# Block 2's first weight chunk split earlier, two modulation units moved ahead, low-part terms last in a three-term product

## The chip, the cores and the metric

The kernel runs on one core of a Trainium2 chip. The metric is the device time of one execution in microseconds (us). The engines are named as in the profile: PE is the matrix engine (PEld its weight loads), DVE the vector engine, ACT the scalar engine, POOL the general-purpose engine, SP the queue that issues nearly all loads.

## The reference, cut to what matters

Two blocks run one after the other on 256 tokens of width 1024 in float32. The first block ends in a mixture of 32 experts, two per token. The second block has two layers; each starts with a normalisation that is scaled and shifted by a modulation vector, and a product with `w_in`.

```python
for e in range(N_EXPERTS):                                   # end of block 1
    he = jax.nn.silu(h @ w_gate[e]) * (h @ w_up[e])
    y = y + comb[:, e:e + 1] * (he @ w_down[e])
x = rms_norm(x + y, final_norm_g)
...
c_act = jax.nn.silu(c)
for l in range(DEPTH_2):                                     # block 2, two layers
    mod = c_act @ w_ada[l] + b_ada[l]
    shift, scale, gate = jnp.split(mod, 3, axis=-1)
    h = rms_norm_2(x, norm_g[l]) * (1.0 + scale[:, None, :]) + shift[:, None, :]
    u = h @ w_in[l]
    rg_x, rg_z, ml_x, ml_o, ml_z = jnp.split(u, split_pts, axis=-1)
    ...
    x = x + gate[:, None, :] * (y @ w_out[l])
```

## The kernel before, in words

**Products in three terms.** Activations and weights are split into a high part (rounded to the fast float32 format) and a low part (the rest). A product is the sum high times high, high times low and low times high, so that each tile costs three matmuls (`mm3`, lines 265 to 272). A weight chunk of 1 MB (`col_chunk`, 1024 rows by 256 columns) is split by `split_cols` in two units of 128x1024: ACT copies the high part (`wh`, line 282) and DVE subtracts it (`wl`, line 283). Three buffers each hold `wh` and `wl`. The last chunk of a stage, which is needed right after it, is split into two buffers of the weight pool instead; such tiles are called `wo`.

**Weight buffers.** The pool `wp` has 8 buffers of 1 MB and serves nearly all loads; the pool `we` has 5 more and lives only as long as the experts. Expert weights come in 96 chunks of 1 MB, six for a pair of experts: four of gate and up weights (`g`), two of down weights (`d`). They are dealt over 17 buffers in turn: 5 of `we`, 8 of `wp`, 4 others. The last six chunks (two of pair 15's gate and up chunks, the two down chunks of pair 14 and the two of pair 15) lie in `wp`. Their loads are kept in program order on SP.

**The expert stage.** There are 16 pairs. For each, PE multiplies the gathered tokens with gate and up weights (line 1165), ACT and DVE form the hidden values (lines 1169 and 1170), PE turns them (line 1114) and multiplies them with the down weights (line 1122), ACT and DVE split the result (lines 1124 and 1125), and PE scatters it back to tokens (`back`, line 1135), where DVE adds it to `x1` (line 1137).

**From experts to block 2.** After the pairs, `head_load(0)` loads block 2's first weight chunk into `wp` and splits it into two `wo` buffers (4 splits: two on ACT, two on DVE). The last `back` adds to `x1`; `head_scale` takes for each half of the tokens (i = 0, 1) two sums of squares on ACT (line 365) and two weighted sums on DVE (line 330), and the scale follows on DVE and POOL (lines 331 to 333 and 373). Sixteen matmuls without use for the result (`warm(16)`, line 355) stand behind the last `back` on PE, then one modulation unit. Then `Head(0)` scales `x1` to `xn` (lines 1228 and 1230), PE turns it (line 1236), and `evac` applies the modulation and splits the result in `hh` and `hl` (lines 1250 to 1261). Then `tm_product` computes the first product of block 2 for i = 0 and 1 (`gz0`, line 1291).

**Modulation units.** `ada_unit` computes 512 of the 3072 columns of `mod` of one layer: two 1 MB loads, 8 matmuls of 32 output rows each, which the trace records as 16 (line 401), and a copy on ACT (line 403). `ada_fold` adds four partial rows with 4 small matmuls, recorded as 8 (line 421), and writes shift and scale for the head with one or two small DVE operations (lines 423 and 425). Units 0 to 3 of a layer are folded and must be ready before that layer's head, units 4 and 5 feed the gate. Layer 1's unit 0 runs in the gap between experts and block 2, its units 1, 2 and 3 in layer 0's last stage (`out_proj`), one `unit()` call after each chunk.

**Products with tokens as the stationary side.** `tm_product(i, f)` serves `gz0` and seven more 256-column chunks in each layer (`gz` and `og`, line 1451). A chunk is used twice, for i = 0 and i = 1, each 24 matmuls over k = 0 to 7; k = 0 to 3 read the chunk's first unit, k = 4 to 7 its second.

**Order.** A planner simulates the program, takes for each engine the earliest ready instruction in program order, and so fixes the order in each engine's queue; `issue_after(x)` ties instructions behind x on their engine. On the chip each engine then takes its queue in that order.

Of the kernel before, what the change touches and what calls it, by code (L numbers as in the profile page):

```python
# [9 lines left out]
F32 = mybir.dt.float32  # L10
# [6 lines left out]
P = 128  # L17
T = 256
D = 1024
KT = 8  # L20
# [158 lines left out]
def model(ctx, tc, A, out, dbg=None):  # L179
# [10 lines left out]
    def nm(s):  # L190
        uid[0] += 1
        return f"{s}_{uid[0]}"

    def psum(tag="mm", bufs=4):
        return pp.tile([P, 512], F32, tag=tag, name=nm(tag), bufs=bufs)
# [56 lines left out]
            TE.matmul(o, lhsT=onesr, rhs=dg[:, 0:n].rearrange("p v t -> p (v t)"), start=j == 0, stop=j == 1)  # L252


    def wload(src, n, rows=P):

        t = wp.tile([P, 2048], F32, tag="w", name=nm("w"))
        shp = list(src.shape)
        v = t[:rows, :n]
        if len(shp) == 3:  # L260
            v = v.rearrange("p (a b) -> p a b", a=shp[1])
        SY.dma_start(out=v, in_=src)
        return t
# [123 lines left out]
    cact = cp.tile([P, KT], F32, name="cact")  # L387
    mods = [cp.tile([P, 16], F32, name=f"mods{l}") for l in range(2)]

    def ada_load(l, c):  # L390
        return [wload(A["w_ada_2"][l][hf * 512:(hf + 1) * 512, c * 512:(c + 1) * 512].rearrange("(k p) c -> p k c", p=P), 2048) for hf in range(2)]

    def ada_unit(pool, l, c, ws=None, a=None):


        if a is None:
            a = pool.tile([P, 512], F32, tag="ada", name=nm("ada"), bufs=2)
        acc = psum()
        for hf, w in enumerate(ws or ada_load(l, c)):
            for k in range(4):  # L400
                r = TE.matmul(acc[32 * k:32 * k + 32, :], lhsT=cact[:, hf * 4 + k:hf * 4 + k + 1].to_broadcast([P, 32]), rhs=w[:, k * 512:(k + 1) * 512],  # L401
                              start=hf == 0, stop=hf == 1)
        S.activation(out=a, in_=acc, func=AF.Copy)
        if ws is None:
            ada_fold()
        if c < 4:
            folds.append((l, c, a))
        else:
            gates.append(a)
        return r  # L410

    folds, gates = [], []

    def ada_fold():

        if not folds:
            return
        l, c, a = folds.pop()
        pt = psum_t()
        for j in range(4):  # L420
            TE.matmul(pt[:, j:j + 1], lhsT=a[:, j * P:(j + 1) * P], rhs=cc("r32"), start=True, stop=True)
        m = mods[l][:, 4 * c:4 * c + 4]
        V.tensor_tensor(out=m, in0=pt[:, 0:4], in1=vc(f"bad{l}", 4 * c, 4), op=OP.add)
        if c in (2, 3):
            V.scalar_tensor_tensor(out=m, in0=m, scalar=1.0, in1=vc(f"ng{l}", 4 * (c - 2), 4), op0=OP.add, op1=OP.mult)
# [60 lines left out]
    def eloads(n):  # L486
        while nslot[0] < min(n, len(chunks)):
            eload()
# [477 lines left out]
    with moe, tc.tile_pool(name="mo", bufs=1, reuse_waits="tile") as bp:  # L966
# [173 lines left out]
            return r  # L1140

        for pair in range(NP):
            eloads(6 * pair + 23)
            ws = loaded["g", pair]
            xg = xgs[pair]

            slot = cc("slot")[:, pair:pair + 1]
            oa = bp.tile([P, T], F32, tag="oa", name=nm("oa"))
            ohs = bp.tile([P, T], F32R, tag="ohs", name=nm("ohs"), bufs=3)
            wsl = bp.tile([P, 2], F32, tag="wsl", name=nm("wsl"), bufs=2)  # L1150
            for j in range(2):
                V.scalar_tensor_tensor(out=oa, in0=bc[:, j, :], scalar=slot, in1=bc[:, 2 + j, :], op0=OP.is_equal, op1=OP.mult, accum_out=wsl[:, j:j + 1])
            V.tensor_tensor(out=wsl[:, 0:1], in0=wsl[:, 0:1], in1=wsl[:, 1:2], op=OP.add)
            V.tensor_scalar(out=oa, in0=bc[:, 0, :], scalar1=slot, scalar2=None, op0=OP.is_equal)
            V.scalar_tensor_tensor(out=ohs, in0=bc[:, 1, :], scalar=slot, in1=oa, op0=OP.is_equal, op1=OP.add)

            gu = psum_a()
            for k in range(KT):
                for q in range(2):
                    o = q * CAP  # L1160
                    if pair:
                        w = ws[2 * (k // 4) + q][:].rearrange("p (g k c) -> p g k c", g=2, k=4)[:, :, k % 4, :]
                    else:
                        w = ws[k // 2][:].rearrange("p (q g k c) -> p q g k c", q=2, g=2, k=2)[:, q, :, k % 2, :]
                    r = TE.matmul(gu[64 * q:64 * q + 64, :], lhsT=xg[:, k, o:o + CAP], rhs=w, start=k == 0, stop=k == KT - 1)  # L1165
                    if pair < 2 and k + q:
                        tc.keep_in_program_order(r)
            sil = bp.tile([P, T], F32, tag="sil", name=nm("sil"), bufs=2)
            S.activation(out=sil, in_=gu[:, 0:256], func=AF.Silu)  # L1169
            V.scalar_tensor_tensor(out=sil, in0=gu[:, 256:512], scalar=wsl[:, 0:1], in1=sil, op0=OP.mult, op1=OP.mult)  # L1170
            hidden[pair] = sil, ohs
            if pair > 1:
                with tc.issue_after(r.ins) if pair + 1 < NP else ExitStack():
                    back()
            if pair % 2 and pair + 1 < NP:
                xgs[pair + 1], xgs[pair + 2] = gather(onehot((pair + 1) // 2))
            if pair:
                down(pair - 1)
# [3 lines left out]
        g2 = [psum_a(), psum_a()]  # L1182
        for k in range(8):
            TE.matmul(g2[k // 4][:, (k % 4) * P:(k % 4 + 1) * P], lhsT=ident[0:8, k:k + 1].to_broadcast([8, P]), rhs=g, start=True, stop=True)
        head_load(0)
        jk = wp.tile([P, 2048], F32, tag="w", name=nm("jk"))
        back()
        down(NP - 1)
        last = back(lambda i: i or head_scale(0, jk, g2))
        last = warm(16, last, h2h[0][:, 0:4, :])  # L1190
        dump("x1m", x1)


# [1 line left out]
    with tc.tile_pool(name="b2", bufs=1, reuse_waits="tile") as bp, tc.tile_pool(name="sp2", bufs=3, reuse_waits="tile") as sp:  # L1195
# [70 lines left out]
        head = Head(0)  # L1266
        head.norm((0, 0, V), (0, 1, S))
        head.transpose(0)
        head_scale(1, jk[:, 1024:2048], g2)
        head.evac(0)  # L1270
        head.norm((1, 0, V), (1, 1, S))
        head.transpose(1)
        head.evac(1)
        with tc.issue_after(last.ins):
            ada_unit(bp, 1, 0)
        for l in range(_L2):
            hhv, hlv, su = head.hh, head.hl, scales[l]
            units += [(l, 4), (l, 5)]
# [1 line left out]
            dump(f"hT{l}", f32(hhv))  # L1280
            def tm_product(i, f, after=None):
                o = psum()[:, 0:256]
                for k in range(KT):
                    with tc.issue_after(after.ins) if after and k > 3 else ExitStack():
                        mm3(o, 1, lambda _: (hhv[:, k, i * P:(i + 1) * P], hlv[:, k, i * P:(i + 1) * P]) + f(k, 0, 256),
                            start=k == 0, stop=k == KT - 1)
                return o

            gz0 = bp.tile([P, 2, 256], F32, tag="gz0", name=nm("gz0"))
# [266 lines left out]
                V.tensor_tensor(out=gb[:, 512 * n:512 * n + 512], in0=pb, in1=gb[:, 512 * n:512 * n + 512], op=OP.add)  # L1556

            if l == 0:
                units += [(1, 1), (1, 2), (1, 3)]
                head = Head(1)  # L1560
            else:
                gr, fj, xf = a8("gr"), a8("fj"), a8("xf")[:, 0:2 * D].rearrange("p (i d) -> p i d", i=2)
                SY.dma_start(out=gr[:, 0:D], in_=A["rows"][0:1, _ROW["fg"][0]:_ROW["fg"][0] + D].to_broadcast([P, D]))
                fss = bp.tile([P, 2, 4], F32, tag="fss", name=nm("fss"))
# [73 lines left out]
```

## Time and profile before

| | |
|---|---|
| median of 3 runs | 967.88 us (967.02 to 968.38) |
| the profiled execution | 967.82 us |
| its span in the trace | 966.0 us |
| PE busy | 908.2 us, 94% of the span |
| DVE busy | 597.6 us, 62% |
| ACT busy | 461.9 us, 48% |
| loads | 230.22 MB, 238 GB/s over the span |

Times within the trace count from the span's start; 1.82 us of the execution lie outside the span. The experts run from about 250 to 499 us, the gap to block 2 lies at 499 to 511 us, layer 0 reaches to about 740 us and layer 1 to the end.

### The profile page before, as it was taken

How to read it: one execution, taken by the hardware profiler on the slowest of the kernel's cores; microseconds unless marked ns; L12 is line 12 of the kernel's file. 1: busy time of each engine (PE TensorE's matmuls, PEld its weight loads, DVE VectorE, ACT ScalarE, POOL GpSimd, SP SyncE). 2: the span in 40 equal slices, each digit the busy share in tenths (PEclk: the TensorE clock that was granted, in tenths of full speed). 3: DMA queues.
4: the chain of work that ended last, by engine and by line, in shares of the span. 5: the costliest groups of instructions: out<-in, count | busy, mean ns of one | idle time of the engine just before them, and what ended most of it. 6: DMA issues, size and time to landing. Idle time of an engine off the chain costs nothing.

```text
span 966.0 us, 15088 instructions
## 1 busy us (share of the span) xinstructions
PE 908.2 (94%) x5936; PEld 702.5 (73%) x5936; DVE 597.6 (62%) x1157; ACT 461.9 (48%) x806; POOL 22.6 (2%) x40
## 2 busy tenths in 40 slices
PE   7929998998899999999999999999999999999997
PEld 5928986997444445545448998897787999889776
DVE  5617773484366446445357979446756888935865
ACT  4513564353422112222136778565554678755742
POOL 1000000000100000000000000000100000000100
PEclk9968999998899999999999999999999999999999
DMA  9868479862798999999769753754627954574201
GB/s 317 247 116 287 131 238 360 324 221 79 268 356 328 401 400 400 403 399 404 265 226 310 235 175 131 256 180 143 228 88 242 281 187 163 172 264 174 88 1 44
DMA packets 135014, 230.22 MB, mean 238 GB/s; under 512 B 5784, under 2 KB 79512, under 8 KB 134936
## 3 DMA queue, kind: packets, MB, share of 16 engines
q1 hardware_dynamic: 132280, 227.00, 68.3%
q10 hardware_dynamic: 2656, 2.17, 0.7%
q8 instruction: 49, 0.80, 0.4%
q14 instruction: 29, 0.24, 0.1%
HBM read 226.53 MB, written 2.62 MB: 237 GB/s over the span
## 4 chain that ended last, share of the span: by engine, by line
PE 61%; DVE 4%; issue 3%; ACT 3%; POOL 1%; POOLq 0%; DVEq 0%; ACTq 0%
PE at L1165 11%; PE mm L272 10%; PE mm L271 10%; PE mm L270 10%; PE mm L1122 6%; PE mm L1135 3%; PE mm L1030 3%; PE mm L401 1%; PE mm L1397 1%; DVE wl L283 1%; PE at L1420 1%; ACT wh L282 1%; PE tp L1430 1%; PE at L271 0%; PE at L270 0%
## 5 line engine op out<-in xcount | busy, mean ns | idle before, releaser
L283 DVE TENSOR_TENSOR wl<-w,wh 128x1024 fp32r<-128x1024 f32 x164 | 199.1, 1218 | 122.1 <-ACT wh L282 120.5
L282 ACT ACTIVATE wh<-w 128x1024 fp32r<-128x1024 f32 x164 | 171.8, 1056 | 138.9 <-PE mm L271 76.4
L270 PE MATMUL mm<-hh,wh 128*128 128x256 f32 (+1 forms) x624 | 179.8, 288 | 3.9 <-ACT wh L282 3.3
L272 PE MATMUL mm<-hh,wl 128*128 128x256 f32 (+1 forms) x624 | 178.9, 288 | 0.8 <-DVE wl L283 0.8
L271 PE MATMUL mm<-hl,wh 128*128 128x256 f32 (+1 forms) x624 | 177.1, 284 | 0.9 <-DVE hl L563 0.9
L270 PEld LDWEIGHTS mm<-hh,wh 128*128 128x128 f32 (+1 forms) x624 | 119.4, 191 | 10.0 <-ACT wh L282 5.1
L1165 PE MATMUL at<-w,xg 128*64 128x512 f32 x512 | 122.9, 595 | 0.2 <-PEq L1054 0.2
L272 PEld LDWEIGHTS mm<-hh,wl 128*128 128x128 f32 (+1 forms) x624 | 119.2, 191 | 3.6 <-issue 1.7
L271 PEld LDWEIGHTS mm<-hl,wh 128*128 128x128 f32 (+1 forms) x624 | 119.2, 191 | 2.9 <-issue 1.5
L1165 PEld LDWEIGHTS at<-w,xg 128*64 128x64 f32 x512 | 38.9, 137 | 70.0 <-issue 65.9
L271 PE MATMUL mm<-wl,hh 128*128 128x256 f32 x256 | 72.1, 283 | 0.0
L272 PE MATMUL mm<-wh,hl 128*128 128x256 f32 x256 | 72.0, 283 | 0.0
L270 PE MATMUL mm<-wh,hh 128*128 128x256 f32 x256 | 71.6, 285 | 0.0
L1122 PE MATMUL mm<-w,heT 128*64 128x512 f32 x256 | 63.2, 598 | 0.0
L271 PEld LDWEIGHTS mm<-wl,hh 128*128 128x128 f32 x256 | 48.4, 189 | 2.7 <-issue 2.4
L270 PEld LDWEIGHTS mm<-wh,hh 128*128 128x128 f32 x256 | 47.6, 188 | 3.7 <-issue 2.0
L272 PEld LDWEIGHTS mm<-wh,hl 128*128 128x128 f32 x256 | 48.3, 189 | 1.7 <-issue 1.5
L1137 DVE TENSOR_TENSOR x<-x,mm 128x512 f32<-128x512 f32 x64 | 40.1, 680 | 14.8 <-PE mm L1135 14.8
L1170 DVE SCALAR_TENSOR_TENSOR sil<-at,wsl,sil 128x256 f32<-128x256 f32 x16 | 7.7, 483 | 66.9 <-ACT sil L1169 66.9
L1124 ACT ACTIVATE ys<-mm 128x512 fp32r<-128x512 f32 x32 | 19.1, 597 | 60.8 <-PE mm L1122 60.8
L1169 ACT ACTIVATE sil<-at 128x256 f32<-128x256 f32 x16 | 6.1, 383 | 79.2 <-PE at L1165 79.2
L1122 PEld LDWEIGHTS mm<-w,heT 128*64 128x64 f32 x256 | 18.7, 136 | 31.5 <-issue 28.7
(436 smaller groups left out, 1772.0 us busy)
## 6 DMA issues: line engine op xcount, KB each, us to landing
w<-in_w_in SPq DMA_DIRECT2D x55, 1024.0 KB, 7.5
w<-in_w_down SPq DMA_DIRECT2D x64, 512.0 KB, 10.3
w<-in_w_gate SPq DMA_DIRECT2D x60, 512.0 KB, 10.3
w<-in_w_up SPq DMA_DIRECT2D x60, 512.0 KB, 10.4
w<-in_w_ada SPq DMA_DIRECT2D x24, 1024.0 KB, 5.2
w<-in_w_out SPq DMA_DIRECT2D x20, 1024.0 KB, 5.0
w<-in_w_gate SPq DMA_DIRECT2D x8, 256.0 KB, 7.6
w<-in_w_up SPq DMA_DIRECT2D x8, 256.0 KB, 7.6
```

Source lines behind the costliest of these rows:

```text
L270: pin(TE.matmul(o, lhsT=lh, rhs=rh, start=start and k == 0, stop=False))
L271: pin(TE.matmul(o, lhsT=lh, rhs=rl, start=False, stop=False))
L272: pin(TE.matmul(o, lhsT=ll, rhs=rh, start=False, stop=stop and k == nk - 1))
L282: splits[S] = S.activation(out=h, in_=src, func=AF.Copy)
L283: splits[V] = V.tensor_tensor(out=l, in0=src, in1=f32(h), op=OP.subtract)
L401: r = TE.matmul(acc[32 * k:32 * k + 32, :], lhsT=cact[:, hf * 4 + k:hf * 4 + k + 1].to_broadcast([P, 32]), rhs=w[:, k * 512:(k + 1) * 512] ...
L1030: TE.matmul(ps[:, 256 * a:256 * a + 256], lhsT=part[i][:, k, :], rhs=oht[:, i, :], start=n == 0, stop=n == 3)
L1122: TE.matmul(po[64 * q:64 * q + 64, :], lhsT=heT[:, f * P + 64 * q:f * P + 64 * q + 64], rhs=wd[n][:, (2 * q + f) * 512:(2 * q + f + 1) * 5 ...
L1124: S.activation(out=y[:, 0, :], in_=po, func=AF.Copy)
L1135: r = TE.matmul(ps, lhsT=ohs[:, i * P:(i + 1) * P], rhs=y[:, part, :], start=part == 0, stop=part == 1)
L1137: V.tensor_tensor(out=xs, in0=xs, in1=ps, op=OP.add)
L1165: r = TE.matmul(gu[64 * q:64 * q + 64, :], lhsT=xg[:, k, o:o + CAP], rhs=w, start=k == 0, stop=k == KT - 1)
```

## The change

Four edits. `head_load(0)` moves from behind the last pair to the start of pair 12, ahead of the loads that this pair asks for. The scratch tile `jk` moves from `wp` to `we`, and its second half is replaced by a tile of the head. In the gap, layer 1's units 0 and 1 are computed, with their loads into `we`, both ahead of a shortened `warm(6)`; their copies and folds follow the head; units 2 and 3 are left to `out_proj`. `tm_product` now issues for all k the terms high times high and high times low, and after these the terms with the tokens' low part.

```diff
@@ for pair in range(NP)
+            if pair == NP - 4:
+                head_load(0)
             eloads(6 * pair + 23)
@@ after the last pair
-        head_load(0)
-        jk = wp.tile([P, 2048], F32, tag="w", name=nm("jk"))
+        jk = we.tile([P, 2048], F32, tag="w", name=nm("jk"))
+
+        uu = [nexts.pop(0) for _ in range(2)]
+        uw = [ada_load(*u, pool=we) for u in uu]
         back()
         down(NP - 1)
         last = back(lambda i: i or head_scale(0, jk, g2))
-        last = warm(16, last, h2h[0][:, 0:4, :])
+        ua = [psum(), psum()]
+        for a, ws in zip(ua, uw):
+            for hf, w in enumerate(ws):
+                with tc.issue_after(last.ins):
+                    last = ada_mm(a, w, hf)
+        last = warm(6, last, h2h[0][:, 0:4, :])
@@ head of layer 0
-        head_scale(1, jk[:, 1024:2048], g2)
+        head_scale(1, head.junk[:, 1024:2048], g2)
...
-        with tc.issue_after(last.ins):
-            ada_unit(bp, 1, 0)
+        for u, a in zip(uu, ua):
+            ada_end(bp, *u, a)
+            ada_fold()
@@ def tm_product(i, f, after=None)
+                ts = slice(i * P, (i + 1) * P)
                 for k in range(KT):
                     with tc.issue_after(after.ins) if after and k > 3 else ExitStack():
-                        mm3(o, 1, lambda _: (hhv[:, k, i * P:(i + 1) * P], hlv[:, k, i * P:(i + 1) * P]) + f(k, 0, 256),
-                            start=k == 0, stop=k == KT - 1)
+                        for j, part in enumerate(f(k, 0, 256)):
+                            TE.matmul(o, lhsT=hhv[:, k, ts], rhs=part, start=k + j == 0, stop=False)
+                for k in range(KT):
+                    with tc.issue_after(after.ins) if after else ExitStack():
+                        TE.matmul(o, lhsT=hlv[:, k, ts], rhs=f(k, 0, 256)[0], start=False, stop=k == KT - 1)
@@ end of layer 0
-                units += [(1, 1), (1, 2), (1, 3)]
+                units += nexts
```

`ada_unit` is cut in two: `ada_mm` holds the matmuls, `ada_end` the copy; `nexts` is the list of layer 1's units 0 to 3, and `wload` and `ada_load` take a pool.

## Rows read from the trace of the kernel before

**Rows 1.** Busy time by stretch: PE, PEld, DVE, ACT, POOL; then granted clock, DMA share, GB/s
```profile
505.00:511.00 6.00, 2.58 (x19) 2.11 (x19) 5.02 (x16) 5.07 (x12) 1.49 (x4) 1.00 1.07 360
...
600.00:640.00 40.00, 40.00 (x335) 34.53 (x328) 21.21 (x28) 22.80 (x31) 0.00 (x0) 1.00 0.71 237
...
700.00:735.00 35.00, 35.00 (x207) 27.36 (x206) 20.36 (x24) 16.18 (x21) 0.62 (x2) 1.00 0.28 92
740.00:745.00 5.00, 3.16 (x17) 2.99 (x16) 3.00 (x8) 1.89 (x6) 1.00 (x2) 0.71 1.10 349
```

**Rows 2.** The chain that ended last, in the gap: start, length, what
```profile
502.26 1.82 DVE jk L330 x6
...
505.17 0.70 POOL scales L373
```

**Rows 3.** PE in order of time, gap to first product: start, us, [idle before <-releaser]
```profile
498.83 3.90 PE L355 MATMUL tp<-h2h,onesr 128*128 128x512 f32 x16
502.66 1.92 PE L401 MATMUL mm<-w,cact 128*32 128x512 f32 x16
506.44 0.66 PE L1236 MATMUL tp<-cst,xn 128*128 128x128 f32 x4 [1.87 <-DVE xn L1230]
...
509.02 0.38 PE L270 MATMUL mm<-wo,hh 128*128 128x256 f32 x1 [0.60 <-DVE hh L1258]
...
510.90 0.39 PE L272 MATMUL mm<-wo,hl 128*128 128x256 f32 x1 [1.37 <-DVE hl L1261]
...
516.56 0.27 PE L272 MATMUL mm<-wo,hl 128*128 128x256 f32 x1
```

**Rows 4.** DVE in order of time: the two low-part splits in the gap
```profile
498.71 1.22 DVE L283 TENSOR_TENSOR wo<-w,wo 128x1024 fp32r<-128x1024 f32 x1
...
501.04 1.22 DVE L283 TENSOR_TENSOR wo<-w,wo 128x1024 fp32r<-128x1024 f32 x1
```

**Rows 5.** ACT in order of time, at pair 15
```profile
483.65 0.38 ACT L1169 ACTIVATE sil<-at 128x256 f32<-128x256 f32 x1 [10.74 <-PE at L1165]
```

**Rows 6.** SP in order of time: the last expert loads
```profile
454.67 9.62 SPq L483 DMA_DIRECT2D w<-in_w_down  x8
```

**Rows 7.** DMA issues of the page: KB each, median us to landing
```profile
w<-in_w_down SPq DMA_DIRECT2D x64, 512.0 KB, 10.3
```

**Rows 8.** PE in order of time: pair 15's down product
```profile
492.55 3.65 PE L1122 MATMUL mm<-w,heT 128*64 128x512 f32 x16
```

**Rows 9.** PE in order of time: layer 0's folds and units, layer 1's transposes
```profile
607.77 1.05 PE L421 MATMUL tp<-cst,ada 128*128 128x1 f32 x8
...
728.55 1.92 PE L401 MATMUL mm<-w,cact 128*32 128x512 f32 x16
...
733.15 1.84 PE L421 MATMUL tp<-cst,ada 128*128 128x1 f32 x16
...
742.10 1.07 PE L1236 MATMUL tp<-cst,xn 128*128 128x128 f32 x4 [1.84 <-DVE xn L1230]
```

**Rows 10.** DVE in order of time, end of layer 0
```profile
731.96 0.68 DVE L1581 TENSOR_TENSOR fin<-mm,gb 128x512 f32<-128x512 f32 x1
732.68 0.75 DVE L1584 SCALAR_TENSOR_TENSOR x<-x,scales,fin 128x512 f32<-128x512 f32 x1
...
735.52 1.37 DVE L1252 TENSOR_SCALAR junk<-tp,mods 128x128 f32<-128x128 f32 x4
```

**Rows 11.** ACT in order of time, `og` chunks of layer 0
```profile
624.73 0.39 ACT L1451 ACTIVATE og<-mm 128x256 f32<-128x256 f32 x1 [1.12 <-PE mm L272]
626.14 1.06 ACT L282 ACTIVATE wh<-w 128x1024 fp32r<-128x1024 f32 x1 [1.03 <-PE mm L272]
627.55 0.39 ACT L1451 ACTIVATE og<-mm 128x256 f32<-128x256 f32 x1 [0.35 <-PE mm L272]
...
631.93 0.38 ACT L1451 ACTIVATE og<-mm 128x256 f32<-128x256 f32 x1 [0.36 <-PE mm L272]
633.25 0.39 ACT L1451 ACTIVATE og<-mm 128x256 f32<-128x256 f32 x1 [0.94 <-PE mm L272]
```

**Rows 12.** DVE in order of time, the low part of the same unit
```profile
627.23 1.23 DVE L283 TENSOR_TENSOR wl<-w,wh 128x1024 fp32r<-128x1024 f32 x1 [4.78 <-ACT wh L282]
```

More of the change, by code (lines that the diff above doesn't have):

```diff
@@ L252, in spread, with wload @@
             TE.matmul(o, lhsT=onesr, rhs=dg[:, 0:n].rearrange("p v t -> p (v t)"), start=j == 0, stop=j == 1)
-    def wload(src, n, rows=P):
-        t = wp.tile([P, 2048], F32, tag="w", name=nm("w"))
+    def wload(src, n, rows=P, pool=None):
+        t = (pool or wp).tile([P, 2048], F32, tag="w", name=nm("w"))
         shp = list(src.shape)
@@ L388, in model, with ada_load, ada_mm, ada_end @@
     mods = [cp.tile([P, 16], F32, name=f"mods{l}") for l in range(2)]
-    def ada_load(l, c):
-        return [wload(A["w_ada_2"][l][hf * 512:(hf + 1) * 512, c * 512:(c + 1) * 512].rearrange("(k p) c -> p k c", p=P), 2048) for hf in range(2)]
+    def ada_load(l, c, pool=None):
+        return [wload(A["w_ada_2"][l][hf * 512:(hf + 1) * 512, c * 512:(c + 1) * 512].rearrange("(k p) c -> p k c", p=P), 2048, pool=pool) for hf in range(2)]
     def ada_unit(pool, l, c, ws=None, a=None):
+        acc = psum()
+        for hf, w in enumerate(ws or ada_load(l, c)):
+            r = ada_mm(acc, w, hf)
+        if ws is None:
+            ada_fold()
+        ada_end(pool, l, c, acc, a)
+        return r
+    def ada_mm(acc, w, hf, pin=lambda r: r):
+        for k in range(4):
+            r = pin(TE.matmul(acc[32 * k:32 * k + 32, :], lhsT=cact[:, hf * 4 + k:hf * 4 + k + 1].to_broadcast([P, 32]), rhs=w[:, k * 512:(k + 1) * 512],
+                              start=hf == 0, stop=hf == 1))
+        return r
+    def ada_end(pool, l, c, acc, a=None):
         if a is None:
             a = pool.tile([P, 512], F32, tag="ada", name=nm("ada"), bufs=2)
[L398 to L402, printed above, removed]
         S.activation(out=a, in_=acc, func=AF.Copy)
-        if ws is None:
-            ada_fold()
         if c < 4:
@@ L409, in ada_unit @@
             gates.append(a)
-        return r
     folds, gates = [], []
+    nexts = [(1, c) for c in range(4)]
     def ada_fold():
@@ L1273, in model @@
         head.evac(1)
-        with tc.issue_after(last.ins):
-            ada_unit(bp, 1, 0)
+        for u, a in zip(uu, ua):
+            ada_end(bp, *u, a)
+            ada_fold()
         for l in range(_L2):
```

## The prediction

> **What bounds the kernel now.** I read the stretch table first, then PE in order of time. In the `gz` and `og` chunks of layer 0 and in its last stage PE is busy in every one of the 40 and 35 us [rows 1]: there a matmul taken away is time gained, and a wait added on PE is time lost. The gap between experts and block 2 is different: from 505 to 511 us PE is busy for 2.58 of 6 us, DVE and ACT for 5.02 and 5.07 [rows 1]. The chain that ended last runs there through DVE's weighted sums and POOL's power to the scaled tokens [rows 2], and PE waits three times, 1.87 us before the transposes, 0.60 us for `hh`, 1.37 us for `hl` [rows 3]. So the gap is a chain on DVE with 3.84 us of waits on PE, and what is before and behind it is PE's.
>
> The last `gz0` matmul starts at 516.56 [rows 3]. My model of PE from 498.83 on: 16 `warm` matmuls 3.83 us (498.83 to 502.66), the unit 1.92, the transposes 1.98 (506.44 to 508.42, where the 0.60 us wait begins), 3.84 us of waits, and 48 matmuls of `gz0`. Two chunk ends of `og` lie 627.55 and 633.25 apart [rows 11], 5.70 us for 48 matmuls, 0.119 us each. The sum is 17.27 us and ends at 516.1, close enough.
>
> **The first chunk's split, moved.** In the gap it costs DVE two operations of 1.22 us in the middle of the chain [rows 4]; these 2.44 us go. In pair 15 ACT sits idle for 10.74 us while PE multiplies [rows 5], and DVE waits in the same stretch for ACT's result, so four splits of 1.06 to 1.22 us are covered there. Without the cover, a split in front of line 1169 or 1124 delays PE by its own length at most, some 1.2 us.
>
> Its load of 1 MB now stands on SP ahead of the last seven chunks. A down load of half that size is issued each 1.2 us (9.62 us for eight [rows 6]), so the queue behind it slips by about 2.4 us. The last down load is issued at about 464 and lands 10.3 us later [rows 6, 7], 474; it is used from 492.55 on [rows 8]. The slip is hidden by 18 us. But `wp` has 8 buffers, and the head's chunk, its two split tiles and six expert chunks are nine: one chunk, probably pair 15's last, must wait until the split has read the head's chunk. If the split runs within ACT's idle time, before 483.65, the chunk lands by 494.0 at the latest, and its half of the product starts at 492.55 plus 1.8. I cost it at nothing, with 2.0 us as the upper bound (below).
>
> **The gap, new.** PE's work there: 6 `warm` matmuls 1.44 (6/16 of 3.83), two units 3.84, transposes 1.98, two folds 1.84 (as in [rows 9], 1.84 for two), `gz0` 5.70; together 14.80, which ends at 513.6 without any wait. That is the best case, 2.5 us earlier than 516.1. With all 3.84 us of waits as before it would be 517.5, 1.4 us later: the worst. How much wait stays? Units and `warm` end at 504.1. The scaled tokens, before at about 506.4, come 2.4 us earlier without the splits, 504.0: no long wait before the transposes. The wait for `hh` can be filled with the folds, and the one for `hl` goes, since 16 terms with `hh` per half (1.90 us) now stand ahead of the first with `hl`. Against this: ACT has one copy more, and the planner may put folds ahead of the transposes. I take 1.0 us of wait: 514.6, **-1.5 us**.
>
> **What is left out later.** One fold (0.92) goes from the `gz` stage, at 607.77 [rows 9], where PE is never idle: **-0.9**; 0 if it stood in a wait. In layer 0's last stage one unit and one fold go, 2.84 us of PE. Not all of it can be had: DVE's operation for the next output half starts at 731.96 and its sum at 732.68, ending at 733.43 [rows 10], and these follow a split of `wo` that doesn't move. The next head's operation at 735.52 can come at best some 0.4 us after that, 733.8. I take **-1.7**, between 0 and -2.8.
>
> **The terms' order in the other chunks.** Here the edit can hurt. In program order a chunk's first unit was last read by the 36th of 48 matmuls, 1.43 us before the chunk's end; the split into the freed buffer started at 626.14 (after a wait for PE) and its low part at 627.23, ending at 628.46 [rows 11, 12], 0.91 us after the chunk's end at 627.55. Now the last read is the 44th matmul, 0.48 us before the end, 0.95 later; so the unit would be ready 1.86 us into the next chunk. In program order the first low weight of this unit is now wanted after 9 matmuls, 1.07 us: a wait of 0.8 us in each of 14 chunks, 11.2 us. But the planner doesn't keep program order: between the two outputs of a chunk lie 2.82 us in one chunk and 1.32 us in the next [rows 11], so where the second unit was late it let i = 1 read the first unit meanwhile. With that, 16 matmuls (1.90 us) need only the first unit, and the wait is about nothing. The chunk of 1.32 us is the nearest row; I take 0.05 us for each, **+0.7**, between 0 and 11.2.
>
> For `gz0` of layer 1, four low-part matmuls (0.48) move from before PE's 1.84 us wait [rows 9] to behind it, and short waits for `hl` go: **+0.2**, between -0.3 and +0.7.
>
> Sum: -1.5 - 0.9 - 1.7 + 0.7 + 0.2 = -3.2. Against the profiled execution's 967.82 this is **964.6 us**; that execution is 0.06 us below the median of 967.88, so the same number stands for the median.
>
> **The clock.** Between 740 and 745 us the granted clock was 0.71, between 505 and 511 us 1.00 [rows 1]; in both PE had waited about as long, 1.84 and 1.87 us [rows 9, 3], and four transposes took 1.07 there and 0.66 here. So a wait of this length doesn't always lower the clock. [...]
>
> [...]
>
> **Rivals and chances.** The bound within which a measurement can't be told from no change is 0.2%, 1.9 us.
> - *As summed*: 963.0 to 966.6. Chance 0.42, most of it faster.
> - *Better*: PE has no wait in the gap, and the last stage gives all of 2.8: 964.6 - 1.0 - 1.1 - 0.7 = 961.8. For it: each cover above. Chance 0.16.
> - *The gap gives nothing*: folds and the second unit get in the way of the transposes, so that the waits stay: 964.6 + 2.9 = 967.5. For it: PE gets 1.2 us more of real work there. Against: DVE's chain is shorter by 2.44. Chance 0.18, no change.
> - *The clock falls in the gap*: 964.6 + 1.5 = 966.1 or, with the gap's waits half back, 967.5. For it: the 742 us row. Against: PE's waits get shorter. Chance 0.08.
> - *Slower: the reordered product starves PE.* The place is each of the 14 later chunks, the price 0.8 us each if the planner keeps program order: 964.6 - 0.7 + 11.2 = 975.1. It decides from 0.28 us a chunk, where it eats all 3.9 us of gain; the kernel is slower by over 1.9 us from 0.42. For it: `wh` is freed 0.95 us later. Against: the alternating 2.82 and 1.32 us. Chance 0.11.
> - *The last expert chunk comes late*: if the split stands behind line 1170, its buffer comes free at about 486, the chunk lands at 496.3, 2.0 us late: 966.6. Chance 0.05.
>
> Range: 961.0 to 968.8 leaves out the starved product and the corner where every bound falls well, about 2 in 10. Faster 0.55 (0.35 of the sum's 0.42, the better case, and a little of the others), same 0.29, slower 0.16.
>
> **What would show it.** In the profile after: no `wo` split on DVE between 496 and 505 us, the four of them before pair 15's line 1169; the first transposes at about 504 instead of 506.44; `gz0`'s last matmul near 514.6; no fold at about 607; one unit and one fold fewer ahead of layer 1's transposes, and these near 739 instead of 742.10. In the `og` chunks, PE without waits on `wl`, and 5.70 us from chunk to chunk; 6.1 or more would make the prediction wrong, and so would transposes that still start at 506.

## The result, and the profile after

The changed kernel takes 977.13 us (median of 5 runs, 974.26 to 977.64), the kernel before 968.38 us beside it (5 runs, 967.02 to 969.08): ratio 1.0082, interval 1.0063 to 1.0102. It is 8.75 us slower; I had forecast 964.6 us, 961.0 to 968.8. Its profiled execution is the median, 977.13.

Where the two traces part, by the start of the same instruction in each (us; `xf` by its end). `xr`, `sw`, `pk` and `xf` are tiles that each run writes in this order; they serve as marks of time only:

| | before | after | shift |
|---|---|---|---|
| pair 15's SiLU (ACT) | 483.65 | 489.68 | +6.0 |
| scaled tokens, first half (DVE `xn`) | 505.90 | 506.54 | +0.6 |
| scaled tokens, second half | 506.56 | 513.30 | +6.7 |
| first `xr` evacuation, layer 0 | 523.17 | 532.83 | +9.7 |
| first `sw` copy, layer 0 | 592.80 | 601.64 | +8.8 |
| `pk`, layer 0 | 654.61 | 664.56 | +10.0 |
| first `xr` evacuation, layer 1 | 756.09 | 761.79 | +5.7 |
| first `sw` copy, layer 1 | 824.10 | 829.92 | +5.8 |
| `pk`, layer 1 | 884.24 | 894.85 | +10.6 |
| last `xf` | 962.60 | 972.00 | +9.4 |

So 6 us are lost before the gap, the gap gives 5.4 back up to the first half's tokens and loses 9 from there on; the end of layer 0 gives some 4 back; and layer 1 loses 5 between the `sw` copies and `pk`.

SP in order of time, after; it answers to [rows 6]:
```profile
450.72 0.77 SPq L491 DMA_DIRECT2D w<-in_w_up  x1
465.43 6.23 SPq L262 DMA_DIRECT2D w<-in_w_ada  x3
471.71 0.50 SPq L491 DMA_DIRECT2D w<-in_w_gate  x1
...
473.68 10.66 SPq L491 DMA_DIRECT2D w<-in_w_down  x8
485.10 0.46 SPq L262 DMA_DIRECT2D w<-in_w_ada  x1
```
Three of the four loads of the modulation units stand in SP's order ahead of the last six expert chunks, and nothing is issued from 451.5 to 465.4. SP's waits from 440 to 500 us (in total, times, the longest) say for what:
```profile
SPq L262 <- PE at L1175: 16.2, 2, 13.9
```
One load of a unit (L262) waits 13.9 us for PE's product of a pair (L1175), which must release the buffer of `we` that the load fills. The eight down loads start at 473.68 instead of 454.67.

PE in order of time, after, pair 15 and the gap; it answers to [rows 3, 8]:
```profile
481.28 1.73 PE L1175 MATMUL at<-w,xg 128*64 128x512 f32 x2 [2.11 <-DMA w<-in_w_up]
483.72 5.49 PE L1175 MATMUL at<-w,xg 128*64 128x512 f32 x13 [0.71 <-DMA w<-in_w_up]
...
502.70 3.64 PE L406 MATMUL mm<-w,cact 128*32 128x512 f32 x32
506.27 1.67 PE L355 MATMUL tp<-h2h,onesr 128*128 128x512 f32 x6
507.77 0.60 PE L1253 MATMUL tp<-cst,xn 128*128 128x128 f32 x4
509.80 0.66 PE L1253 MATMUL at<-cst,xn 128*128 128x128 f32 x4 [1.43 <-DVE junk L330]
511.45 1.46 PE L1305 MATMUL mm<-wo,hh 128*128 128x256 f32 x8 [0.99 <-DVE hh L1275]
513.78 1.11 PE L1253 MATMUL at<-cst,xn 128*128 128x128 f32 x4 [0.87 <-ACT xn L1245]
...
518.74 1.10 PE L429 MATMUL tp<-cst,ada 128*128 128x1 f32 x8
...
520.40 1.05 PE L429 MATMUL tp<-cst,ada 128*128 128x1 f32 x8 [0.34 <-DVE junk L1269]
```
PE waits for expert weights in pair 15, and in the gap for DVE and ACT between the two halves. Four transposes of the second half take 1.11 us, the first four of the first half 0.60. The stretch table, after, columns as in [rows 1]:
```profile
480.00:500.00 20.00, 18.01 (x67) 6.63 (x67) 5.13 (x8) 2.56 (x5) 0.00 (x0) 0.83 1.05 384
500.00:510.00 10.00, 8.45 (x52) 3.87 (x53) 6.84 (x19) 4.80 (x12) 0.77 (x2) 1.00 1.10 349
510.00:520.00 10.00, 8.13 (x44) 7.46 (x42) 4.29 (x15) 8.10 (x15) 0.77 (x2) 0.66 0.54 171
```
The granted clock is 0.83 from 480 to 500 us, where pair 15 waits, and 0.66 from 510 to 520 us, behind the waits of the gap; before, it was 1.00 in all three stretches. By estimate from this row, at most 0.34 of the 10 us, 3.4 us, is lost to it.

ACT in order of time, after, at the two halves of the head:
```profile
506.54 0.72 ACT L1245 ACTIVATE xn<-x,scales 128x512 f32<-128x512 f32 x1 [1.99 <-POOL scales L373]
507.97 0.63 ACT L365 ACTIVATE junk<-x 128x512 f32<-128x512 f32 x1 [0.71 <-PE tp L355]
...
513.00 0.72 ACT L1245 ACTIVATE xn<-x,scales 128x512 f32<-128x512 f32 x1 [0.34 <-POOL scales L373]
```
The squares of the second half (L365) go into `head.junk`; they stand behind the first half's scaled tokens and wait 0.71 us for PE's `warm` (L355), which reads `h2h`, the memory that `head.junk` takes over. `x1`'s second half was ready at 504.4.

ACT, after, `og` chunks of layer 0, against [rows 11]:
```profile
635.04 0.36 ACT L1473 ACTIVATE og<-mm 128x256 f32<-128x256 f32 x1
635.30 1.05 ACT L282 ACTIVATE wh<-w 128x1024 fp32r<-128x1024 f32 x1
638.72 0.39 ACT L1473 ACTIVATE og<-mm 128x256 f32<-128x256 f32 x1 [2.37 <-PE mm L1308]
640.01 1.06 ACT L282 ACTIVATE wh<-w 128x1024 fp32r<-128x1024 f32 x1 [0.91 <-PE mm L1308]
640.98 0.37 ACT L1473 ACTIVATE og<-mm 128x256 f32<-128x256 f32 x1
641.24 1.06 ACT L282 ACTIVATE wh<-w 128x1024 fp32r<-128x1024 f32 x1
644.66 0.38 ACT L1473 ACTIVATE og<-mm 128x256 f32<-128x256 f32 x1 [2.37 <-PE mm L1308]
```
The two splits of a chunk now come together, 1.2 us apart, and a chunk takes 5.94 us (638.72 to 644.66) instead of 5.70.

### The profile page after: what moved, and what is told of

The parts are those of the page before. It is cut to its first block, busy times and chain, and to the rows that moved or that the text cites. A ratio compares the mean times of both kernels' runs of the same rounds, so it can differ in the third digit from the quotient of the medians.

```text
span 975.4 us, 15066 instructions
## 1 busy us (share of the span) xinstructions
PE 913.9 (94%) x5926; PEld 706.0 (72%) x5926; DVE 598.3 (61%) x1157; ACT 458.3 (47%) x804; POOL 22.1 (2%) x40
## 4 chain that ended last, share of the span: by engine, by line
PE 40%; issue 27%; ACT 3%; DVE 2%; POOL 1%; POOLq 0%; ACTq 0%; DVEq 0%
PE mm L272 7%; PE mm L271 7%; PE mm L270 7%; PE mm L1305 7%; PE mm L1308 3%; PE mm L1419 1%; PE mm L406 1%; ACT wh L282 1%; PE at L1442 1%; DVE wl L283 1%; PE tp L1452 1%; PE at L271 0%; PE at L270 0%; PE at L272 0%; PE tp L1577 0%
## 5 line engine op out<-in xcount | busy, mean ns | idle before, releaser
L1175 PE MATMUL at<-w,xg 128*64 128x512 f32 x512 | 127.1, 606 | 3.1 <-DMA w<-in_w_up 2.8
L1175 PEld LDWEIGHTS at<-w,xg 128*64 128x64 f32 x512 | 39.6, 139 | 76.5 <-issue 70.7
L1305 PE MATMUL mm<-wl,hh 128*128 128x256 f32 x224 | 54.2, 281 | 0.0
L1305 PE MATMUL mm<-wh,hh 128*128 128x256 f32 x224 | 53.7, 287 | 0.1
L1305 PEld LDWEIGHTS mm<-wh,hh 128*128 128x128 f32 x224 | 40.4, 188 | 4.4 <-issue 2.9
L1305 PEld LDWEIGHTS mm<-wl,hh 128*128 128x128 f32 x224 | 41.6, 188 | 1.2 <-DVE it L1407 0.8
L1133 DVE TENSOR_TENSOR ys<-mm,ys 128x512 fp32r<-128x512 f32 x32 | 22.1, 690 | 25.1 <-ACT ys L1132 25.0
L1143 PEld LDWEIGHTS mm<-ys,ohs 128*128 128x128 f32 x128 | 22.5, 188 | 19.7 <-issue 12.2
```

The costliest lines, as they stand in the source:

```text
L1133: V.tensor_tensor(out=y[:, 1, :], in0=po, in1=f32(y[:, 0, :]), op=OP.subtract)
L1143: r = TE.matmul(ps, lhsT=ohs[:, i * P:(i + 1) * P], rhs=y[:, part, :], start=part == 0, stop=part == 1)
L1305: TE.matmul(o, lhsT=hhv[:, k, ts], rhs=part, start=k + j == 0, stop=False)
```

## The experiments

Each was run beside the kernel before, whose median moved between 967.05 and 968.08 from one set of runs to the next; so the table has the difference to it (before's own median beside it in brackets), and differences between kernels are differences of these. The intervals are 2 to 6 us wide; a difference of 1 us between two rows is not told apart. The traces of e3 and g2 are of their fastest executions (966.53 and 967.51, their medians 969.43 and 970.87): there the trace shows the order of things, and the median the price.

| | kernel | median us | to before | interval of the ratio |
|---|---|---|---|---|
| e1 | changed; unit loads behind the experts | 974.98 | +6.9 (968.08) | 1.0063 to 1.0106 |
| e2 | changed; `warm` reads other memory | 980.45 | +12.4 (968.08) | 1.0084 to 1.0141 |
| e3 | before; new order everywhere | 969.43 | +1.4 (968.08) | 1.0003 to 1.0026 |
| e4 | e1 + e2, new order in `gz0` alone | 967.66 | -0.4 (968.08) | 0.9983 to 1.0006 |
| e5 | before; new order in `gz0` alone | 966.04 | -1.0 (967.05) | 0.9980 to 1.0008 |
| e6 | e4; `warm` 16 | 964.24 | -2.8 (967.05) | 0.9956 to 0.9977 |
| e7 | e4; folds later | 963.69 | -3.4 (967.05) | 0.9950 to 0.9976 |
| e8 | before; split moved, alone | 964.09 | -3.0 (967.05) | 0.9946 to 0.9975 |
| e9 | changed; new order in `gz0` alone | 972.88 | +4.9 (968.00) | 1.0036 to 1.0077 |
| e10 | e6; unit loads ahead again | 970.33 | +2.3 (968.00) | 1.0012 to 1.0041 |
| e11 | e6; folds later | 965.27 | -2.7 (968.00) | 0.9961 to 0.9981 |
| e12 | e8 + e5 | 963.96 | -4.0 (968.00) | 0.9944 to 0.9976 |
| g1 | e3; low part last within each unit | 965.93 | -1.9 (967.80) | 0.9973 to 0.9995 |
| g2 | before; modulation part alone | 970.87 | +3.1 (967.80) | 1.0021 to 1.0045 |
| g3 | changed; `warm` 16 | 977.90 | +10.1 (967.80) | 1.0090 to 1.0128 |
| h1 | e4; `jk` in `wp`, second half's scratch in it, `warm` on `h2h` | 962.11 | -5.8 (967.88) | 0.9931 to 0.9957 |
| h2 | h1; `warm` 16 | 965.16 | -2.7 (967.88) | 0.9963 to 0.9987 |
| h3 | h1; folds later | 963.30 | -4.6 (967.88) | 0.9937 to 0.9969 |

**The unit loads in SP's queue: e1, e4, e10.** The four loads are held to their place in program order (`keep=True` makes `wload` do so), behind the expert loads, which are held so already:
```
-    uw = [ada_load(*u, pool=we) for u in uu]
+    uw = [ada_load(*u, pool=we, keep=True) for u in uu]
```


> The changed kernel with one thing different: the four loads of the two modulation units stand behind the last six expert chunks in SyncE's order, where three of them stood ahead. Theory Q (the unit loads hold up the expert chunks, because SyncE waits at them for the buffers of pair 14): the SiLU of pair 15 falls from 489.7 back to about 483.7, its products show no wait for w_up above 0.3 us, and 3.5 to 6 us come back: 971 to 973.5. Rival G (the loads are late but the loss is made in the gap by the units' own late arrival): the pair is early again but the units' products now wait for their loads, the first transposes stay near 507.8, and under 2 us come back: 975.5 or more.

The SiLU of pair 15 came back to 484.08, but the median by 1.9 us only, outside what either theory gave. At the first `xr` evacuation e1 is 5.6 us ahead of the changed kernel, at layer 1's first `xr` 2.5: from layer 0's `pk` to there the changed kernel takes 97.2 us, e1 99.2 and the kernel before 101.5. Why the changed kernel is short there is not shown. With the other faults mended the price is easier to read. e4 has two more edits (e2's, and the old order of terms behind `gz0`, where `pre` is a new parameter that asks for the new order, and `wot` holds the split tiles of block 2's first chunk):
```
-    last = warm(6, last, h2h[0][:, 0:4, :])
+    last = warm(6, last, wot[0][0][0][:, 0:512])
...
-    S.activation(out=gz0[:, i, :], in_=tm_product(i, heads[l], None if i else head.turned), func=AF.Silu)
+    S.activation(out=gz0[:, i, :], in_=tm_product(i, heads[l], None if i else head.turned, pre=True), func=AF.Silu)
```


> The changed kernel with three edits: the unit loads behind the expert chunks, the warm matmuls on the split chunk, and the new order of terms kept for gz0 alone (the other chunks of tm_product as in the kernel before). If theories Q, J and T are each right and add up: -4.5, -2 and -3.5 us from 977.1, about 967, level with or a little under the kernel before. If they share the same 9.4 us in part (the same wait mended twice), 969 to 972. If one is wrong, above 972.

e10 is e6 (e4 with 16 `warm`) without `keep=True`.

> The kernel of e6 (964.2 us) with one mending undone: the unit loads are ahead of the last six expert chunks again. Theory Q: the SiLU of pair 15 is late again, 489 to 490 instead of 483.7, and the whole of it, 5 to 6 us, is seen at the first xr evacuation and at the end: 968.5 to 970.5. Rival, from e1, where mending it gave back only 2.2 us of the median: 966 to 967.5.

ACT at pair 15, in e6 and then in e10:
```profile
483.34 0.38 ACT L1184 ACTIVATE sil<-at 128x256 f32<-128x256 f32 x1 [8.85 <-PE at L1180]
```
```profile
489.97 0.38 ACT L1182 ACTIVATE sil<-at 128x256 f32<-128x256 f32 x1 [16.01 <-PE at L1178]
```
e10 is 5.1 us slower than e6 (+2.3 against -2.8), for 6.6 us at this row. The queue costs about 5 us here; e10's executions lie from 966.5 to 972.8. Why the planner put the loads there was not tried. In g2, which has the same loads but the split behind the experts, they stand behind the last down load.

**The scratch of the second half: e2, g2, h1.** e2 has the first edit of e4 alone.

> The changed kernel with one thing different: the six warm matmuls read the first 512 columns of block 2's split chunk instead of the gathered activations h2h, whose memory head.junk takes over. Same count and size of matmuls. Theory J (the squares of the second token half wait for the end of the warm matmuls through that shared memory): the squares of head_scale(1) start at about 505 to 506.3 instead of 507.97, the second transposes at about 511 to 512 instead of 513.78, and 1.5 to 3 us come back: 974 to 975.6. Rival: the squares wait for ScalarE's own work or for another reader of that memory, and the time stays within 1 us of 977.1.

The wait for `warm` went (the squares at 506.87), and nothing was won: the squares still stood behind the first half's scaled tokens, DVE still put four evacuations between the two weighted sums, and the second half's tokens came at 512.58. The theory of a wait for `warm` fell. The 3.6 us that e2 is above the changed kernel are, by its trace (of its slowest execution, 981.19), not lost in the gap: its first `xr` comes at 532.46, against 532.83, and layer 1's first `xr` at 765.57, against 761.79. g2 has the modulation part of the change in the kernel before, with nothing of the split or the new order.

> The kernel before with the modulation part alone: two units ahead of the first transposes, 6 warm matmuls, both folds in the gap, head.junk as scratch; the split stays behind the experts and the terms keep their old order. Theory: in the gap the second unit and the folds cost 1.9 and 1.8 us of PE and the lower clock up to 3; a fold in the gz stage (0.9) and the end of layer 0 (1.7) come back: 968 to 971, with a granted clock under 0.9 between 505 and 520 us. Rival, the prediction's: the waits of the gap take them in, 964.5 to 966.

It loses 3.1 us without any late load; the second half's tokens come 6.1 us behind the first's (504.38 and 510.51), 0.7 before. The clock stood at 0.85 between 510 and 520 us. Left over was where the scratch lies. h1 is e4 with these edits, and with `warm` on `h2h` again:
```
-    jk = we.tile([P, 2048], F32, tag="w", name=nm("jk"))
+    jk = wp.tile([P, 2048], F32, tag="w", name=nm("jk"))
...
-    head_scale(1, head.junk[:, 1024:2048], g2)
+    head_scale(1, jk[:, 1024:2048], g2)
```


> The kernel of e4 (967.7 us: loads behind the experts, new order in gz0 alone), but the second half's squares use the other half of the tile jk, which comes from the weight pool as in the kernel before, and the 6 warm matmuls read h2h again. Theory S (head.junk is the cause): the scaled tokens of the second half come 0.7 us behind the first's instead of 4.3, PE's wait of 1.95 us before the transposes goes, and the clock of 500 to 520 us stays at 0.9 or more: 963 to 965. Rival: the second unit and folds set the gap, the scaled tokens come early but gz0 ends as late: 966.5 to 968.

ACT's squares of the second half in e4, and then in h1, followed by PE in the gap of h1:
```profile
501.02 0.72 ACT L1250 ACTIVATE xn<-x,scales 128x512 f32<-128x512 f32 x1 [2.00 <-POOL scales L378]
501.65 0.61 ACT L370 ACTIVATE junk<-x 128x512 f32<-128x512 f32 x1
...
504.97 0.72 ACT L1250 ACTIVATE xn<-x,scales 128x512 f32<-128x512 f32 x1 [1.03 <-POOL scales L378]
```
```profile
499.18 0.64 ACT L367 ACTIVATE jk<-x 128x512 f32<-128x512 f32 x1 [0.48 <-DVE x L1147]
...
499.81 0.61 ACT L367 ACTIVATE jk<-x 128x512 f32<-128x512 f32 x1
...
502.77 1.39 ACT L1247 ACTIVATE xn<-x,scales 128x512 f32<-128x512 f32 x2 [2.26 <-POOL scales L375]
```
```profile
503.32 0.66 PE L1255 MATMUL tp<-cst,xn 128*128 128x128 f32 x4
...
505.53 1.02 PE L431 MATMUL tp<-cst,ada 128*128 128x1 f32 x8 [0.24 <-DVE junk L1271]
506.81 1.02 PE L431 MATMUL tp<-cst,ada 128*128 128x1 f32 x8 [0.25 <-DVE junk L1271]
...
512.49 1.09 PE L1311 MATMUL mm<-wo,hl 128*128 128x256 f32 x8
```
In e4 the squares wait for nothing, and yet stand behind the first half's scaled tokens, though `x1`'s second half was ready at 498.9. In h1 they run as soon as `x1`'s half is added, ahead of the first scaled tokens; the second half's tokens are 0.66 us behind; PE waits 0.5 us in all, and the clock is 1.00 from 500 to 520 us. h1 is 5.4 us below e4, and all of it is there at the first `xr` (520.17 against 525.60). Its other two edits don't explain this: with `jk` in `we`, the first half's squares of e4 run at 495.90, with `jk` in `wp`, those of h1 at 496.77; and the operand that h1 takes back had made e2 0.4 us earlier, not later, at the first `xr`. The memory in which the second half's squares land was the fault, through the order that ACT and DVE got, more than through the wait.

**The order of terms: e3, e5, e9, g1.** e3 is the diff's `tm_product` in the kernel before, e5 with `pre=True` for `gz0` and the old order behind it.

> The kernel before with the new order of terms in tm_product alone (low part of the tokens last), everything else as before. The prediction's term: +0.7 us over 14 chunks, 0.05 each: about 969. Theory T, from the shifts between the two traces (layer 1's chunks of gz and og lose about 3.5 us from 812 to 883): +3 to +5 us in all, 971.5 to 973.5, with chunks of og 5.9 us apart instead of 5.7 and later weight splits on VectorE. If the second stage is what the loss of that stretch hangs on rather than the order, the time stays within 1 us of 968.4.

> The kernel before with the new order of terms in the two gz0 products alone, all other chunks as before. In the run with the new order everywhere the first xr evacuation came 2.9 us earlier than before, and the loss began only behind the sw copies (2.0 us in layer 0, 4.8 us in layer 1). Theory: the order is a gain in gz0, where PE waits for hl, and a loss in the chunks where a unit of the split weights is freed later. Then nothing is given back here: 963 to 965.5. Rival: the early start is only one execution's luck with the clock; then 967 to 968.5.

e9 is the changed kernel with e5's edit.

> The changed kernel with one thing different: the new order of terms stays in gz0 alone, the other chunks of tm_product have the order of the kernel before. In the trace of the changed kernel the shift to before grows by 1.1 us from sw to pk in layer 0 and by 4.8 us in layer 1; in the kernel with the new order alone by 2.0 and 4.8. Theory T (the order costs this in any surroundings): 5 to 7 us come back, 970 to 972. Rival (most of it is how the late loads and the order meet): under 3 us come back, above 974.

Behind `gz0` the new order costs 2.4 us in the kernel before (e3 to e5) and 3.9 in the changed one (to e9). Both are below what the theory gave: in e3 `gz0`'s gain is set off against it, and e9's 3.9 lies between theory and rival. e9's shift to before no longer grows from `sw` to `pk` (+6.2 to +5.3 in layer 0, +5.2 to +5.2 in layer 1). What is at fault in the order, g1 tells; it keeps the low part last, but within a unit:
```
+                for k0 in range(0, KT, per):
+                    for k in range(k0, k0 + per):
...
+                            TE.matmul(o, lhsT=hhv[:, k, ts], rhs=part, start=k + j == 0, stop=False)
+                    for k in range(k0, k0 + per):
...
+                            TE.matmul(o, lhsT=hlv[:, k, ts], rhs=f(k, 0, 256)[0], start=False, stop=k == KT - 1)
```
`per` is 8 in `gz0` and 4 behind it.

> As e3 (the kernel before, new order of terms everywhere; 969.4 us), but behind gz0 the low part comes last within each unit of four k instead of within the whole chunk: 8 high terms, 4 low terms, 8 high, 4 low. A unit's last read is then where it was in the kernel before. Theory B (the loss is that both units of a chunk come free together, so that the two splits into them follow one another): no loss, as in e5, 965.5 to 967, and og evacuations 5.70 us from chunk to chunk. Rival (the order itself or its weight loads cost PE time): the chunks stay at 5.9 us, 968.5 to 970.

ACT's `og` chunks of layer 1, first e3, then g1:
```profile
865.60 1.06 ACT L282 ACTIVATE wh<-w 128x1024 fp32r<-128x1024 f32 x1 [0.90 <-PE mm L1290]
866.56 0.36 ACT L1455 ACTIVATE og<-mm 128x256 f32<-128x256 f32 x1
866.82 1.05 ACT L282 ACTIVATE wh<-w 128x1024 fp32r<-128x1024 f32 x1
```
```profile
863.63 1.06 ACT L282 ACTIVATE wh<-w 128x1024 fp32r<-128x1024 f32 x1 [0.32 <-PE mm L1291]
865.03 0.38 ACT L1456 ACTIVATE og<-mm 128x256 f32<-128x256 f32 x1 [0.34 <-PE mm L1291]
865.31 1.05 ACT L282 ACTIVATE wh<-w 128x1024 fp32r<-128x1024 f32 x1
867.95 1.06 ACT L282 ACTIVATE wh<-w 128x1024 fp32r<-128x1024 f32 x1 [1.59 <-PE mm L1291]
```
In e3 both units of a chunk are read to its end, and their splits come as a pair; in g1 they are spread again, as before, and 3.2 us are gone (+1.4 to -1.9), with as many matmuls as in e3. So the price lay in when the buffers come free, not in the matmuls. Layer 1's first `gz` chunk shows it too, ACT in e3 and then in e5:
```profile
831.69 1.06 ACT L282 ACTIVATE wh<-w 128x1024 fp32r<-128x1024 f32 x1 [1.43 <-PE mm L1290]
```
```profile
827.16 1.05 ACT L282 ACTIVATE wh<-w 128x1024 fp32r<-128x1024 f32 x1
```
In e3 ACT waits 1.43 us for PE before it can split into the first freed buffer; in e5 it doesn't wait.

**Clock, `warm` and folds: e6, e7, e11, g3, h2, h3.** `warm(6, ...)` becomes `warm(16, ...)` in e6, g3 and h2; in e7, e11 and h3 the loop behind the second evacuation ends without `ada_fold()`, and the folds run in the `gz` stage.

> The kernel of e4 with 16 warm matmuls instead of 6. In e4 the granted clock of 500 to 520 us was 0.74, where the kernel before has 1.00. [...] Rival: the length of warm has no part in it; the clock stays at 0.74 to 0.85 and the 2.4 us of ten more warm matmuls push part of the gap back: 967.5 to 970.

> The kernel of e4 with the two folds left out of the gap (they run in the gz stage, as the one fold of the kernel before did). In e4 the folds take 1.7 us each at the lower clock in the gap. Theory F (the folds stand on PE's path ahead of the second transposes and gz0): the first xr evacuation comes 1.5 to 3.4 us earlier than in e4 and 1.8 us are given back in the gz stage, where PE is never idle: 966 to 967.5. Rival: they fill a wait for hh, as the prediction has it; the xr evacuation stays and the gz stage is 1.8 us longer: 968.5 to 969.5.

> The kernel of e4 with both 16 warm matmuls and the folds left to the gz stage; alone they gave back 3.4 and 4.0 us. Theory: both act on the same thing, PE at the lower clock in the gap, so together they give little more than one: 963 to 964.5. Rival: the folds also cost their own length in the gap, 0.9 us each at full clock, of which the gz stage takes back less; then 961.5 to 963.

> The changed kernel with 16 warm matmuls instead of 6, nothing else. If the short warm costs in these surroundings what it costs in e4: 3.4 us come back, 973 to 974.5, with the clock at 0.95 or more between 510 and 520 us. If the late scaled tokens of the second half leave PE waiting there all the same: the clock stays under 0.85, the ten matmuls also hold up the squares that wait for warm, and the time is 976.5 to 979.

> h1 with 16 warm matmuls instead of 6. If h1 has no wait and no lower clock left, the ten matmuls cost their 2.4 us of PE: about 2 us above h1. If the clock still falls in h1, they win it back, and h2 is 1 to 3 us below h1.

> h1 with the two folds left to the gz stage. If the gap of h1 is PE work at full clock, the folds move from one busy stretch to another: within 1 us of h1. If the folds still stand on the path at the lower clock, 1.5 to 3.5 us below h1.

PE in the gap of e4:
```profile
505.75 1.03 PE L1258 MATMUL at<-cst,xn 128*128 128x128 f32 x4 [1.95 <-ACT xn L1250]
...
507.42 1.71 PE L434 MATMUL tp<-cst,ada 128*128 128x1 f32 x8
```
Behind the wait for the late second half PE is at the lower clock (0.79 from 500 to 510 us, 0.69 from 510 to 520), and a fold takes 1.71 us, for 1.02 in h1 at 1.00. By estimate from these two clocks, at most 2.1 and 3.1 us, 5.2 in sum, are lost to it. Ten more `warm` matmuls (e6, -2.4 us, clock 1.00 in both stretches, against its rival's 0.74 to 0.85) or no folds (e7, -2.9, 0.83 and then 1.00) mend this; both (e11, 1.00 in both) give no more than one. Where the wait is gone (h1), the same edits cost 3.1 (h2) and 1.2 us (h3, whose interval meets h1's). In the changed kernel, with its longer waits, 16 `warm` were no gain (g3, +1.4; the clock of 510 to 520 us was 1.00, that of 520 to 530 us 0.83).

In h2 the ten matmuls are only part of the loss. PE in `gz0` of h1, then of h2, and h2's stretch, columns as in [rows 1]:
```profile
507.69 3.07 PE L1308 MATMUL mm<-wo,hh 128*128 128x256 f32 x24
```
```profile
508.94 4.61 PE L1308 MATMUL mm<-wo,hh 128*128 128x256 f32 x24
```
```profile
510.00:520.00 10.00, 10.00 (x76) 10.00 (x76) 4.54 (x5) 4.22 (x6) 0.39 (x2) 0.87 0.96 310
```
The transposes start 1.3 us later than in h1, and 24 matmuls of `gz0` take 1.5 us longer: the clock fell to 0.87 with 16 `warm` where it stayed at 1.00 with six, behind the same two waits of 0.24 and 0.25 us. So in e4 the short `warm` and the folds cost what the late scaled tokens made of them; in h1 neither is a fault.

**The split alone: e8, e12.**
```
     for pair in range(NP):
+        if pair == NP - 4:
+            head_load(0)
```
with `head_load(0)` behind the loop taken out. e12 adds e5's edit.

> The kernel before with one part of the change: the first chunk's load and split ahead of the last four expert pairs; one unit, 16 warm matmuls and the old order of terms stay. The prediction: the loads behind it slip by 2.4 us, which is hidden, and DVE's chain in the gap is 2.44 us shorter, so that the first transposes come at about 504 to 504.5 instead of 506.4; 966 to 967. If the slip or the splits hold up pair 15, its SiLU comes later than 483.65 and the time is above 968.1. If the gap's chain doesn't hang on the splits, 967.5 to 968.5.

> The kernel before with the split ahead of the last pairs and the new order in gz0 alone, one unit and 16 warm matmuls: the two parts of the change that cost nothing by themselves (964.1 and 966.0 us, before 967.1). If they add up: 962 to 963.5. If the order only fills waits that the early split already takes away (0.74 us of wait for hl are left in e8): 963.5 to 964.5.

PE in the gap of e8:
```profile
503.42 0.66 PE L1237 MATMUL tp<-cst,xn 128*128 128x128 f32 x4 [0.47 <-DVE xn L1231]
...
507.51 0.38 PE L272 MATMUL mm<-wo,hl 128*128 128x256 f32 x1 [0.74 <-DVE hl L1262]
```
The transposes come 3.0 us earlier, with pair 15 on time (SiLU 484.09), and the median falls by 3.0. By the differences to before, e12 (-4.0) is the sum of e8 (-3.0) and e5 (-1.0); but its median is that of e8 (963.96 and 964.09), and the intervals don't tell the two readings apart.

## Why the prediction was wrong, point by point

- **The split, moved.** Right in its mechanism. The chain from pair 15's SiLU to the first scaled tokens is 18.78 us in e8 instead of 22.25, so 3.5 us shorter where I had 2.44. The buffer that waits for the split exists: in e4, e6 and e8 the eight down loads stretch over 25 us, and pair 15 is not late.
- **"I cost it at nothing", the queue.** This step failed. It counted the head's chunk on SP, 2.4 us hidden by 18, but not the four unit loads of 1 MB into `we` that the same change moves ahead. Three stood ahead of six expert chunks, and SP waited at them for PE: 5.1 us (e6 to e10).
- **The gap, new.** The sum of PE's work was sound: in h1, which has both units, six `warm` and both folds in the gap, PE takes 15.5 us from the units' start (498.06) to the end of `gz0` (513.6), where I had 14.8 without waits and 15.8 with 1.0 us of them. That 513.6 is the very figure of my best case is luck: the stretch starts 0.8 us earlier than I counted. So h1's first `xr` is 3.0 us ahead of the kernel before, where I forecast 1.5. The step that failed is that I took the second half's scaled tokens to come with the first's. The diff moves their scratch into the next block's memory, and the prediction has no sentence on it: 5.4 us (e4 to h1), the lower clock and the slow folds within it.
- **The terms' order.** This term was mis-sized. I named the mechanism and its place, then priced it at 0.7 us because the planner could let `i = 1` read the first unit meanwhile; with both units read to the chunk's end that didn't cover it. Measured in the trace of e3 against before: from `og` chunk to `og` chunk 0.25 us more in layer 0 and 0.3 in layer 1, some 0.8 and 1.0 over three; 1.7 more from the end of the last `og` to `pk` in each layer (9.6 us before, 11.3 in e3 and in the changed kernel); and from `sw` to the first `og` 2.1 more in layer 1, lost at its first `gz` chunk, and 0.4 less in layer 0. That is 2.0 and 4.8 us in sum. The stages behind `pk` give part of it back, and 2.4 (e3 to e5) or 3.9 (changed to e9) stay by the medians. The rival's rule (0.28 a chunk eats the gain) was near; its 975.1 is near the result only by chance, since two other faults make up most of the loss.
- **Folds and end of layer 0.** Right. In h1 the shift goes from -3.54 at `sw` to -4.43 at the last `gz`, -0.9 as forecast. From `pk` to the first half's tokens of layer 1 h1 takes 75.71 us instead of 74.63, from these to the second half's 9.47 instead of 12.23: -1.7 in sum, as forecast.
- **`gz0` of layer 1.** Not told apart: e5's -1.0 covers both layers, and its interval reaches 1.
- **The clock.** It fell, as one rival had it, but neither a shorter `warm` nor late tokens explain it alone. The rival's 1.5 us is an estimate from [rows 1]: a clock of 0.71 over 5 us is 0.29 of 5 us lost; no run shows that loss by itself. From 510 to 520 us, with the second half's tokens late, the clock was 0.66 and 0.69 with six `warm` (the changed kernel, e4) and 1.00 with sixteen (g3, e6; in g3 it was 0.83 from 520 to 530 us); with these tokens on time it was 1.00 with six (h1) and 0.87 with sixteen (h2). Its cause stays open.

The three prices, 5.1 for the queue, 5.4 for the scratch and 3.9 for the order, sum to 14.4, and from the changed kernel (+8.75) to h1 (-5.8) it is 14.5. The sum agrees, but each price was taken in other surroundings, and alone they don't all show: mending the queue in the changed kernel (e1) gave 1.9. h1 is the change without the three, and beats both kernels: 962.11 us, ratio 0.9944, interval 0.9931 to 0.9957. Why e1 gave so little, and why e2 lost 3.6 behind layer 0's `pk`, stays open; executions of e2 lie from 973.3 to 981.2.

## What to carry to other kernels

For each load that an edit adds or moves, write down the buffer it takes and what stands behind it on its queue: here one early load that had to wait 13.9 us on SP made the eight down loads behind it start at 473.68 instead of 454.67. Scratch counts as an edge too: with the second half's scratch in memory that another phase still reads, ACT and DVE got an order in which its scaled tokens came 6.1 us behind the first half's (g2), instead of 0.7. And a new order of reads is priced by when each buffer is read last: in e3 two came free together, their splits on ACT followed one another, 1.22 us apart, and an `og` chunk took 0.25 to 0.3 us more.

## What the runs showed of the hardware

Ten more matmuls without use made one kernel faster, where PE came from a wait of 1.95 us (e4 to e6: 2.4 us less), and another slower, where PE had work at once (h1 to h2: 3.1 us more, half of it in 24 matmuls that took 4.61 us instead of 3.07, at a granted clock that fell only with the ten more). And the length of a wait doesn't tell the clock: in h3 PE waits 1.76 us for `hh`, and the clock is 1.00 from 500 to 520 us, while in h2, behind waits of 0.24 and 0.25 us, it is 0.87 from 510 to 520 us. From 735 to 745 us, where the second half's transposes of layer 1 lie, PE is idle for 2.8 us in e3 and in e4, and the clock is 1.00 in the one and 0.83 in the other. Each of these is one profiled execution; what decides is not shown.
